# One decoder layer on one core: the first attention reads, the last head's sums and the last conv output pieces change places

## The chip, the cores and the metric

The kernel runs on one core of a Trainium2 chip. The metric is the time of one execution on the device in microseconds (us), as the median of several runs. A core has five engines with instruction queues of their own: PE (TensorE, matmuls and transposes), DVE (VectorE), ACT (ScalarE), POOL (GpSimd) and SP, which here issues all the DMAs. They wait for each other by semaphores only. Matmuls read SBUF and write PSUM; the other engines read PSUM and so make a PSUM tile free for the next matmuls.

## The reference

One transformer layer over 1024 tokens of width 1024, float32. Cut to what matters here:

```python
h = rms_norm(x, g_mix)
q, k, v, qi, ki, wi, conv_in, gate_a, gate_c = jnp.split(h @ w_in, pts, axis=-1)
q, k = per-head rms_norm                      # 8 heads of 64
# indexer: scores of every query with every key, the 256 best are kept
rel   = relu(einsum('bqhd,bsd->bqhs', qi, ki) * 64 ** -0.5)
idx   = top_k(where(causal, einsum('bqhs,bqh->bqs', rel, wi), -inf), 256)
# attention of each query over its selected keys, 8 heads
attn  = softmax(where(valid, q . k[idx] * 64 ** -0.5, -inf)) @ v[idx]
conv  = silu(layer_norm(causal depthwise conv of a * sigmoid(g), 31 taps))
x = x + (sigmoid(gate_a) * (attn @ w_attn_o)
         + sigmoid(gate_c) * (conv @ w_conv_o)) @ w_out
x = x + (silu(hf @ w_gate) * (hf @ w_up)) @ w_down        # hf = rms_norm(x)
x = x + sigmoid(rms_norm(x) @ w_pg) * (p @ w_pp)
```

## The kernel before

Everything is kept transposed, with features on the partitions and the 1024 tokens along the free axis. A large product is done with operands split in two rounded float32 parts (`..hi` and `..lo`), so that one product takes three matmuls of 128x512 (hi by hi, lo by hi, hi by lo). The stages come in this order: projection for the indexer; the search for the 256th score of each query, spread over the following stages; conv input and gates; blocks for k, v and q; attention; the merge of both branches through `w_ao` (attention output) and the gates; `w_out`; feed-forward; the last embedding product.

**q blocks.** Four q blocks (`qk_gemm(0, i)`), two heads each, come one after another. A block's product lies in a pair of PSUM banks (tag `g`, two such pairs). ScalarE squares it (`sq`), ScalarE and VectorE write its two parts `qh` and `ql`, and SP spills them to device memory (`qdh`, `qdl`, 512 KB each). Behind block i the statistics of block i-1 are made: 16 matmuls with `headsel` (L724), `ms` on VectorE, `r` on GpSimd (L205) and two small products on VectorE (`rq`, L730). The order of this part is set by a scheduler, which places each instruction by the time it simulates.

**Attention operands.** `att_prep(j)` (L758) reads the spilled q and k of two heads back, in the layout that the scores want: for each head `qst` (q's two parts one above the other), and two `kst` tiles with k's parts twice. It is 12 DMAs of 64x1024 (256 KB), all from SP, L128. In the kernel before, `att_prep(0)` stands behind q block 2.

**Attention loop.** From L952 the order is written by hand: engines run exactly what the code emits, in that order. A unit is a pair of heads j and a block b of 128 queries; 32 units run in a software pipeline over i from -2 to 32. In step i stand, for each of the two heads u: `scores(u)` of unit i+2 (L787, into a PSUM pair `g`; VectorE adds the mask and takes the maximum into `lg`, L790), a conv output piece, `turn(u)` of unit i (transposes of `lg`, L812, into PSUM tiles of tag `m`, of which there are three; ScalarE and VectorE write them to `pt`, L813 and L814), `values(u)` of unit i-1 (L826, L827) and `exp(u)` of unit i+1 (ScalarE, L802). Then `negmax` (`nmx`), and `finish` of unit i-1: a reciprocal on VectorE, two scaled copies to `osum` on ScalarE (L841), and two sums on GpSimd (L843, L844) that write `attn`. Every four units `att_turn` transposes half a head pair's result (4 transposes, L853) and `att_split` rounds it into `ahi` and `alo` on VectorE (L858, L859) for the merge. The first unit's scores and the statistics of q block 3 open the loop.

**Conv output pieces.** `co_blocks` (L863) is a generator of 64 pieces, each three matmuls into the PSUM tile `f`, of which there is one. Four pieces fill it, then VectorE multiplies it with the gate (`scl`, L881); two such halves make a spill (`cgd`). `pump(co)` emits the next piece: the loop uses them to fill TensorE between the steps (FILL gives how many for each b), and `pump(co, 64)` emits what is left after the loop. Some of those left are placed by the scheduler among the instructions of the loop's end. The matmuls of the merge (tile `g` from `ahi` and `alo`, gate product into `sal`) for the first two outputs are moved up in the same way.

Of the kernel before, what the change touches and what calls it, by code (L numbers as in the profile page):

```python
# [18 lines left out]
ALU = mybir.AluOpType  # L19
# [52 lines left out]
def tile_layer(ctx: ExitStack, tc: tile.TileContext, A, out):  # L72
    nc = tc.nc
    pe, dve, act, pool, sp = nc.tensor, nc.vector, nc.scalar, nc.gpsimd, nc.sync
# [10 lines left out]
    def nm(s):  # L85
        cnt[0] += 1
        return f"{s}_{cnt[0]}"

    def U(name="u", dt=F32, shape=(P, S)):
        return up.tile(list(shape), dt, tag="u", name=nm(name))  # L90
# [12 lines left out]
    def PM(shape=(P, 512)):  # L103
        return mp.tile(list(shape), F32, tag="m", name=nm("m"))
# [14 lines left out]
    def pump(gen, k=1):  # L119
        for _ in range(k):  # L120
            next(gen, None)
# [539 lines left out]
    def v_turn(j, vt):  # L661
        pt = PG()
        for tb in range(8):
            pe.transpose(pt[:, tb * P:(tb + 1) * P], vt[:, tb * P:(tb + 1) * P], ident)
        pv = pt.rearrange("p (t h c) -> p t h c", t=8, h=2)
        r = U("vr")
        rv = r.rearrange("p (t h c) -> p t h c", t=8, h=2)
        for u in range(2):
            vv = U("vall", BF16, (P, 8, VW))
            parts = [vv[:, :, 2 + 64 * i: 66 + 64 * i] for i in range(3)]  # L670
            act.activation(parts[0], pv[:, :, u], AF.Copy)
            dve.tensor_tensor(rv[:, :, u], pv[:, :, u], parts[0], op=ALU.subtract)

            dve.tensor_tensor(vv[:, :, 0:2], rv[:, :, u, 0:2], rv[:, :, u, 0:2], op=ALU.is_equal)
            act.activation(parts[1], rv[:, :, u], AF.Copy)
            dve.tensor_tensor(parts[2], rv[:, :, u], parts[1], op=ALU.subtract)
            vall.append(vv)
# [28 lines left out]
    def qk_gemm(which, j):  # L706
        wt = weights("w_k" if which else "w_q", j)
        ps = PG()
        gemm(halves(ps), wk(wt, 8), hT)
        sq = U("sq")  # L710
        act.activation(sq, ps, AF.Square)
        if which:
            o = U("k")
            act.activation(o, ps, AF.Copy, scale=gqk)
            return sq, o
        hi, lo = U("qh", FR), U("ql", FR)
        split_x(hi, lo, ps)
        to_dram(hi, lo, qd, "qd")
        return sq, None

    def qk_stats(sq):
        st = PM()
        for tb in range(8):
            pe.matmul(st[:, 2 * tb:2 * tb + 2], lhsT=sq[:, tb * P:(tb + 1) * P], rhs=headsel, start=True, stop=True)  # L724
        return rstd_of(st[:, 0:16], 1.0 / HD, 16)

    def q_scales(r):
        for dst, sign in ((rq, 1.0), (nrq, -1.0)):
            t = up.tile([P, 16], F32, tag="rq", name=nm("rq"), bufs=8)
            dve.tensor_scalar(t, r, sign * HD ** -0.5, None, op0=ALU.mult)  # L730
            dst.append(t)
# [24 lines left out]
    def att_prep(j):  # L756
        (qh, ql), (kh, kl) = qd[j], kd[j]
        for u in range(2):  # L758
            rows = slice(64 * u, 64 * u + 64)
            a, b0, b1 = U("qst", FR), U("kst", FR), U("kst", FR)  # L760
            mv(a[0:64], qh[rows])
            mv(a[64:128], ql[rows])
            for o in (0, 64):
                mv(b0[o:o + 64], kh[rows])
                mv(b1[o:o + 64], kl[rows])
            stk[2 * j + u] = a, b0, b1
# [3 lines left out]
    class Unit:  # L770
# [57 lines left out]
                          start=False, stop=(kb == self.b))  # L828
            self.pt[u] = None

        def finish(self):
            j = self.j
            if j not in avs:
                avs[j] = U("attn")
            avv = avs[j].rearrange("p (b h c) -> p b h c", b=8, h=2)
            o2 = self.o[:, 0:2 * VW].rearrange("p (u x) -> p u x", u=2)
            rc = up.tile([P, 2], F32, tag="s2", name=nm("rc"), bufs=12)
            dve.reciprocal(rc, o2[:, :, 0])
            sm = U("osum")[:, 0:6 * HD].rearrange("p (u i c) -> p u i c", u=2, i=3)
            for u in range(2):  # L840
                act.activation(sm[:, u], o2[:, u, 2:VW].rearrange("p (i c) -> p i c", i=3), AF.Copy,  # L841
                               scale=rc[:, u:u + 1])
            pool.tensor_tensor(sm[:, :, 1], sm[:, :, 1], sm[:, :, 2], op=ALU.add)  # L843
            pool.tensor_tensor(avv[:, self.b], sm[:, :, 0], sm[:, :, 1], op=ALU.add)  # L844

    def att_turn(j, half):
        av = avs[j]
        if len(aT) == j:
            aT.append((U("ahi", FR), U("alo", FR)))
        ps = PM()  # L850
        for i in range(4):
            c = half * 512 + i * P
            pe.transpose(ps[:, i * P:(i + 1) * P], av[:, c:c + P], ident)  # L853
        return j, half, ps

    def att_split(j, half, ps):
        hi, lo = (t[:, HV[half]] for t in aT[j])
        dve.tensor_copy(hi, ps)  # L858
        dve.tensor_tensor(lo, ps, hi.bitcast(F32), op=ALU.subtract)  # L859
# [3 lines left out]
    def co_blocks():  # L863
        def fetch(n):
            g = U("scl")
            sp.dma_start(g, spill_g[1, n])
            return g

        nxt = fetch(0)
        for n2 in range(4):  # L870
            wt = weights("w_co", n2)
            for i in range(2):
                n = 2 * n2 + i
                g = nxt
                d = dp.tile([P, S], F32, tag=f"cg{n}", name=nm("cgd"))
                for sl in HV:
                    ps = fp.tile([P, 512], F32, tag="f", name=nm("f"))
                    for k in range(4):
                        gemm([(ps, sl)], wk(wt, 4, off=512 * i), cT, k, k + 1)
                        if k == 3:  # L880
                            dve.tensor_tensor(g[:, sl], g[:, sl], ps, op=ALU.mult)  # L881
                        if sl == HV[1] and k == 0 and n < 7:
                            nxt = fetch(n + 1)
                        yield
                sp.dma_start(d, g)
                spill_c[n] = d
# [55 lines left out]
    for i in range(4):  # L942
        xq[i] = qk_gemm(0, i)
        if i == 0:
            pump(cn_)
            v_turn(3, vt.pop(3))
        else:
            q_scales(qk_stats(xq.pop(i - 1)[0]))
        if i == 2:
            att_prep(0)  # L950
        pump(cn_)
    co = co_blocks()  # L952
    todo = [(j, b) for j in range(4) for b in (range(7, -1, -1) if j % 2 == 0 else range(8))]
    N = len(todo)
    un = {}
    with tc.manual_schedule():
        for i in range(-2, N + 1):
            new, nxt, cur, old = None, un.get(i + 1), un.get(i), un.pop(i - 1, None)
            if i + 2 < N:
                new = un[i + 2] = Unit(*todo[i + 2])  # L960
            if i == 0:
                r3 = qk_stats(xq.pop(3)[0])
            if i == 2:
                q_scales(r3)
            if i % 8 == 2 and i < 24:
                att_prep(i // 8 + 1)
            fill = FILL[cur.b] if 0 <= i < N else 0
            for u in range(2):
                if new:
                    new.scores(u)  # L970
                if u < fill:
                    pump(co)
                if 0 <= i < N:
                    cur.turn(u)
                if old:
                    old.values(u)
                if nxt:
                    nxt.exp(u)
                if u + 2 < fill:
                    pump(co)  # L980
            if new:
                new.negmax()
            if old:
                old.finish()
            if i > 4 and i % 4 == 1:
                j, odd = (i - 5) // 8, (i - 5) % 8 // 4
                att_split(*att_turn(j, (1 - odd) if j % 2 == 0 else odd))
    pump(co, 64)
    att_split(*att_turn(3, 1))


    mhi, mlo, sg_, cg_ = [], [], {}, {}
# [421 lines left out]
```

## Time and profile before

| | |
|---|---|
| median of 3 runs | 1629.14 us (1626.28 to 1632.62) |
| profiled execution | 1629.16 us |
| its span in the trace | 1627.3 us |
| mean granted clock of TensorE | 0.991 |
| TensorE busy | 1590.6 us (98% of the span) |
| VectorE, ScalarE, GpSimd busy | 70%, 44%, 9% |
| DMA moved | 184.69 MB, 113 GB/s on average |

Times in the trace count from the start of the span. The q blocks run from about 493 to 540 us, the attention loop from 540 to 723 us, the merge from there on. Busy time of a group of matmuls is modelled, since they are pipelined: the start of the next group says when it made room. The granted clock is a share of full speed (1.00 is 2.4 GHz, 0.50 is 1.2 GHz). An idle time stands in brackets behind the instruction that ended it, with what released it.

### The profile page before, as it was taken

Reading aid. Unit: us, or ns where it says so; the run is one execution under the profiler, and the core shown is the slowest. Engines: PE = TensorE matmul, PEld = TensorE weight load, DVE = VectorE, ACT = ScalarE, POOL = GpSimd, SP = SyncE. Lnnn points to the kernel's source line nnn. Section 1 sums busy time; section 2 is a strip of 40 time slices with the busy share of each in tenths; the row PEclk is TensorE's granted clock in tenths of the full one; section 3 lists DMA queues with packets and bytes.
Section 4 is the critical chain, followed back from the end, with each engine's and each line's share of the span. In section 5 each row is a group of like instructions: output and inputs, shape, how many; then the busy total and the mean of one; then the engine's idle time right before and its main releaser. Section 6 shows DMA issues by size and latency. Waiting matters only on the chain.

```text
span 1627.3 us, 20334 instructions
## 1 busy us (share of the span) xinstructions
PE 1590.6 (98%) x7736; PEld 1329.4 (82%) x7736; DVE 1140.8 (70%) x1804; ACT 714.2 (44%) x1066; POOL 150.1 (9%) x136
## 2 busy tenths in 40 slices
PE   8999999999999999999999899999999999999998
PEld 6888888888878788878888678888888888888887
DVE  5669999884899778747468876667777544437763
ACT  5456375768733577742234433322322322212531
POOL 2101100000202521221001200000000000000210
PEclk9999999999999899999999999999999999999999
DMA  7330222232221844336542122222222552223254
GB/s 290 95 91 27 65 91 89 94 104 78 91 91 72 225 131 110 103 145 223 210 136 78 59 78 87 93 80 78 78 78 91 182 193 83 99 91 104 92 199 136
DMA packets 61538, 184.69 MB, mean 113 GB/s; under 512 B 7296, under 2 KB 7808, under 8 KB 61440
## 3 DMA queue, kind: packets, MB, share of 16 engines
q1 hardware_dynamic: 61440, 183.38, 33.9%
q8 instruction: 61, 1.00, 0.3%
q14 instruction: 37, 0.30, 0.1%
HBM read 134.60 MB, written 45.09 MB: 110 GB/s over the span
## 4 chain that ended last, share of the span: by engine, by line
PE 52%; DVE 3%; ACT 0%; issue 0%; ACTq 0%; DVEq 0%
PE g L190 41%; PE m L190 10%; DVE xsum L1080 1%; DVE xc L179 0%; DVE wlo L179 0%; DVE wd L1153 0%; PE m L212 0%; DVE h L248 0%; PE f L190 0%; ACT whi L178 0%; DVE sil L1127 0%; PE m L222 0%; ACT one L178 0%; DVE raw L1157 0%; DVE sal L1010 0%
## 5 line engine op out<-in xcount | busy, mean ns | idle before, releaser
L143 ACT ACTIVATE whi<-raw 128x1024 fp32r<-128x1024 f32 x110 | 115.5, 1051 | 199.5 <-PE g L190 182.4
L190 PE MATMUL g<-hhi,whi 128*128 128x512 f32 (+2 forms) x656 | 201.0, 388 | 2.1 <-ACT vt L658 1.5
L190 PE MATMUL g<-hlo,whi 128*128 128x512 f32 (+2 forms) x656 | 199.5, 385 | 2.6 <-POOL hlo L179 1.3
L190 PE MATMUL g<-hhi,wlo 128*128 128x512 f32 (+2 forms) x656 | 199.3, 385 | 0.0
L144 DVE TENSOR_TENSOR wlo<-raw,whi 128x1024 fp32r<-128x1024 f32 x102 | 127.3, 1249 | 44.9 <-ACT whi L143 44.7
L613 DVE SCALAR_TENSOR_TENSOR cacc<-glu,vecs,cacc 128x994 f32<-128x994 f32 (+14 forms) x120 | 151.7, 1264 | 2.7 <-ACT cacc L610 1.9
L511 ACT ACTIVATE junka<-Y,tr 128x1024 bf16<-128x1024 f32 (+3 forms) x128 | 126.3, 987 | 46.0 <-DVE tr L536 23.1
L190 PEld LDWEIGHTS g<-hlo,whi 128*128 128x128 f32 (+1 forms) x656 | 122.2, 187 | 28.0 <-POOL hlo L179 2.1
L190 PEld LDWEIGHTS g<-hhi,whi 128*128 128x128 f32 (+1 forms) x656 | 121.6, 187 | 25.4 <-ACT vt L658 1.9
L190 PEld LDWEIGHTS g<-hhi,wlo 128*128 128x128 f32 (+1 forms) x656 | 122.2, 187 | 24.2
L1292 DVE TENSOR_TENSOR x<-x,g 128x1024 f32<-128x1024 f32 (+1 forms) x56 | 59.8, 1067 | 107.7 <-PE g L190 107.7
L205 POOL TENSOR_TENSOR r<-ms,mhalf 128x16 f32<-128x16 f32 (+2 forms) x14 | 34.8, 2489 | 1036.2 <-DVE ms L203 1020.6
L190 PE MATMUL g<-xc,whi 128*128 128x512 f32 x352 | 109.9, 394 | 4.7 <-DVE sil L1127 3.3
L190 PE MATMUL g<-fah,whi 128*128 128x512 f32 x352 | 113.9, 390 | 0.4 <-ACT phi L178 0.4
L190 PE MATMUL g<-fal,whi 128*128 128x512 f32 x352 | 113.6, 389 | 0.0
L190 PE MATMUL g<-fah,wlo 128*128 128x512 f32 x352 | 113.6, 389 | 0.0
L190 PE MATMUL g<-xc,w 128*128 128x512 f32 x480 | 112.0, 389 | 0.0
L190 PE MATMUL m<-xc,whi 128*128 128x512 f32 x352 | 108.9, 390 | 0.0
L190 PEld LDWEIGHTS g<-xc,w 128*128 128x128 f32 x480 | 90.0, 188 | 18.8 <-ACT w L178 0.2
L190 PEld LDWEIGHTS g<-xc,whi 128*128 128x128 f32 x352 | 66.7, 190 | 19.5 <-DVE sil L1127 3.7
L190 PEld LDWEIGHTS g<-fah,whi 128*128 128x128 f32 x352 | 66.1, 188 | 14.6 <-ACT phi L178 0.7
L814 DVE SCALAR_TENSOR_TENSOR pt<-m,pt 128x512 f16<-128x512 f32 (+3 forms) x96 | 50.6, 554 | 38.9 <-ACT pt L813 38.4
(240 smaller groups left out, 3226.6 us busy)
## 6 DMA issues: line engine op xcount, KB each, us to landing
raw<-w_fd SPq DMA_DIRECT2D x26, 512.0 KB, 3.8
hd<-hd SPq DMA_DIRECT2D x22, 512.0 KB, 4.9
raw<-w_fg SPq DMA_DIRECT2D x40, 256.0 KB, 3.0
raw<-w_fu SPq DMA_DIRECT2D x40, 256.0 KB, 2.9
hd<-c SPq DMA_DIRECT2D x20, 512.0 KB, 2.8
x<-xT SPq DMA_DIRECT2D x16, 512.0 KB, 8.5
sgd<-sg SPq DMA_DIRECT2D x16, 512.0 KB, 2.9
raw<-w_out SPq DMA_DIRECT2D x16, 512.0 KB, 3.8
```

The lines of the kernel that those rows point to most:

```text
L143: act.activation(hi, raw, AF.Copy)
L144: lo_eng.tensor_tensor(lo, raw, hi.bitcast(F32), op=ALU.subtract)
L190: pe.matmul(ps, lhsT=W[k][wi], rhs=X[k][xi][:, sl], start=(k == 0 and t == 0), stop=(k == K - 1 and t == 2))
L205: pool.tensor_tensor(r, ms, mhalf[:, :width], op=ALU.pow)
L511: act.activation(junka[:, :n], ysl(b), AF.Sign, scale=-1.0, bias=self.tr[:, c], accum_out=self.cn[:, c])
L613: dve.scalar_tensor_tensor(acc[:, sl], g, w, acc[:, sl], op0=ALU.mult, op1=ALU.add)
L814: dve.scalar_tensor_tensor(lo[:, c0:c0 + cw], pt[:, :cw], PSCALE, hi[:, c0:c0 + cw], op0=ALU.mult, op1=ALU.subtract)
L1080: dve.tensor_tensor(a, x2[p + k][:, HV[u]], x2[q + k][:, HV[v]], op=op)
L1292: dve.tensor_tensor(x2[n][:, sl], x2[n][:, sl], ps[:, sl], op=ALU.add)
```

## The change

It has three parts. `att_prep(0)` is emitted behind q block 1 instead of q block 2. `finish` gets the engine for its two sums as an argument: GpSimd as before, but VectorE for the last unit. And at the end of the hand-ordered part now stand four conv output pieces, the last `att_turn`, three pieces and the last `att_split`; before, the remaining pieces and both calls stood behind that part.

```diff
@@ -828,7 +828,7 @@
                           start=False, stop=(kb == self.b))
             self.pt[u] = None
 
-        def finish(self):
+        def finish(self, add):
             j = self.j
             if j not in avs:
                 avs[j] = U("attn")
@@ -840,8 +840,8 @@
             for u in range(2):
                 act.activation(sm[:, u], o2[:, u, 2:VW].rearrange("p (i c) -> p i c", i=3), AF.Copy,
                                scale=rc[:, u:u + 1])
-            pool.tensor_tensor(sm[:, :, 1], sm[:, :, 1], sm[:, :, 2], op=ALU.add)
-            pool.tensor_tensor(avv[:, self.b], sm[:, :, 0], sm[:, :, 1], op=ALU.add)
+            add.tensor_tensor(sm[:, :, 1], sm[:, :, 1], sm[:, :, 2], op=ALU.add)
+            add.tensor_tensor(avv[:, self.b], sm[:, :, 0], sm[:, :, 1], op=ALU.add)
 
     def att_turn(j, half):
         av = avs[j]
@@ -946,7 +946,7 @@
             v_turn(3, vt.pop(3))
         else:
             q_scales(qk_stats(xq.pop(i - 1)[0]))
-        if i == 2:
+        if i == 1:
             att_prep(0)
         pump(cn_)
     co = co_blocks()
@@ -981,12 +981,15 @@
             if new:
                 new.negmax()
             if old:
-                old.finish()
+                old.finish(dve if i == N else pool)
             if i > 4 and i % 4 == 1:
                 j, odd = (i - 5) // 8, (i - 5) % 8 // 4
                 att_split(*att_turn(j, (1 - odd) if j % 2 == 0 else odd))
+        pump(co, 4)
+        last = att_turn(3, 1)
+        pump(co, 3)
+        att_split(*last)
     pump(co, 64)
-    att_split(*att_turn(3, 1))
 
 
     mhi, mlo, sg_, cg_ = [], [], {}, {}
```

The first place is SP's queue at q blocks 1 and 2. `qdh_4135` and `qdl_4137` are the spill of block 1; `qdh_4230` and `qdl_4232` that of block 2 in the kernel before. Before:

```order
L128 DMA qdh_4135<-qh_4131 128x1024
L128 DMA qdl_4137<-ql_4132 128x1024
L128 DMA qdh_4230<-qh_4226 128x1024
L128 DMA qst_4251<-qdh_4008 64x1024
L128 DMA qst_4251<-qdl_4010 64x1024
L128 DMA qdl_4232<-ql_4227 128x1024
L128 DMA kst_4252<-kdh_3471 64x1024
...
L128 DMA kst_4262<-kdl_3473 64x1024
L128 DMA qdh_4368<-qh_4364 128x1024
```

After, where `qdh_4248` and `qdl_4250` are the spill of block 2:

```order
L128 DMA qdh_4135<-qh_4131 128x1024
L128 DMA qst_4156<-qdh_4008 64x1024
L128 DMA qst_4156<-qdl_4010 64x1024
L128 DMA qdl_4137<-ql_4132 128x1024
L128 DMA kst_4157<-kdh_3471 64x1024
L128 DMA kst_4158<-kdl_3473 64x1024
...
L128 DMA kst_4167<-kdl_3473 64x1024
L128 DMA qdh_4248<-qh_4244 128x1024
L128 DMA qdl_4250<-ql_4245 128x1024
L128 DMA qdh_4368<-qh_4364 128x1024
```

Two of the twelve reads stand ahead of the second half of block 1's spill, the other ten behind it, and both halves of block 2's spill behind all twelve.

The second place is TensorE at the end of the loop, from the first transposes of the last unit (`m_6667`) on. `chi`, `clo` are the conv branch's operand, `whi`, `wlo` the weights. `pt_6600` is unit 30's, `m_6681` its values. Before, the last unit's transposes, a group of twelve `f` matmuls (its middle left out) and then the values of unit 30:

```order
L190 MATMUL f_6479<-chi_4303,wlo_6000 128x512
L812 MATMUL m_6667<-ident_73,lg_6519 128x128 x4
L812 MATMUL m_6674<-ident_73,lg_6519 128x128 x4
L190 MATMUL f_6773<-chi_4288,whi_5999 128x512
L190 MATMUL f_6773<-clo_4289,whi_5999 128x512
...
L190 MATMUL f_6773<-clo_4304,whi_5999 128x512
L190 MATMUL f_6773<-chi_4303,wlo_6000 128x512
L826 LDWEIGHTS pt_6600
L826 MATMUL m_6681<-vall_4033,pt_6600 128x194
```

After, the same place, and further on in the queue the last four transposes of `attn` (`m_6788`) between two groups of `f`:

```order
L812 MATMUL m_6667<-ident_73,lg_6519 128x128 x4
L812 MATMUL m_6674<-ident_73,lg_6519 128x128 x4
L826 LDWEIGHTS pt_6600
L826 MATMUL m_6681<-vall_4033,pt_6600 128x194
...
L190 MATMUL f_6772<-clo_4304,whi_5999 128x512
L190 MATMUL f_6772<-chi_4303,wlo_6000 128x512
L853 MATMUL m_6788<-ident_73,attn_6294 128x128 x4
L190 MATMUL f_6795<-chi_4288,whi_5999 128x512
...
L190 MATMUL f_6795<-chi_4303,wlo_6000 128x512
L190 MATMUL g_6845<-ahi_6588,whi_6472 128x512
```

The group of twelve between the first transposes and the values of unit 30 is gone from there, and so is another one ahead of unit 31's values. One group now stands ahead of the last four transposes and one between these and the merge's first products from `ahi`. A third one, which stood between those products, comes behind them.

The third place is VectorE there, from the first transposes' copies to the gate products. Before:

```order
L814 SCALAR_TENSOR_TENSOR pt_6666<-m_6667,pt_6666 128x512
L814 SCALAR_TENSOR_TENSOR pt_6666<-m_6674,pt_6666 128x512
L881 TENSOR_TENSOR scl_6346<-scl_6346,f_6773 128x512
L814 SCALAR_TENSOR_TENSOR pt_6696<-m_6697,pt_6696 128x512
L814 SCALAR_TENSOR_TENSOR pt_6696<-m_6704,pt_6696 128x512
L838 RECIPROCAL rc_6725<-m_6681 128x2
L838 RECIPROCAL rc_6765<-m_6732 128x2
L858 CAST ahi_6588<-m_6820 128x512
L881 TENSOR_TENSOR scl_6777<-scl_6777,f_6791 128x512
L859 TENSOR_TENSOR alo_6589<-m_6820,ahi_6588 128x512
L881 TENSOR_TENSOR scl_6777<-scl_6777,f_6805 128x512
L1010 TENSOR_TENSOR sal_6827<-sal_6827,g_6845 128x1024
```

After:

```order
L814 SCALAR_TENSOR_TENSOR pt_6666<-m_6667,pt_6666 128x512
L814 SCALAR_TENSOR_TENSOR pt_6666<-m_6674,pt_6666 128x512
L814 SCALAR_TENSOR_TENSOR pt_6696<-m_6697,pt_6696 128x512
L814 SCALAR_TENSOR_TENSOR pt_6696<-m_6704,pt_6696 128x512
L838 RECIPROCAL rc_6725<-m_6681 128x2
L838 RECIPROCAL rc_6765<-m_6732 128x2
L843 TENSOR_TENSOR osum_6767<-osum_6767 128x2x64
L844 TENSOR_TENSOR attn_6294<-osum_6767 128x128
L881 TENSOR_TENSOR scl_6346<-scl_6346,f_6772 128x512
L858 CAST ahi_6588<-m_6788 128x512
L859 TENSOR_TENSOR alo_6589<-m_6788,ahi_6588 128x512
L881 TENSOR_TENSOR scl_6776<-scl_6776,f_6795 128x512
```

The product L881 between the two pairs of L814 is gone from there, the two sums stand behind the reciprocals, and a L881 stands ahead of `ahi` and behind `alo`.

## Rows read from the trace of the kernel before

**Rows 1.** Page, busy time: us (share of the span), instructions.
```profile
PE 1590.6 (98%) x7736; PEld 1329.4 (82%) x7736; DVE 1140.8 (70%) x1804; ACT 714.2 (44%) x1066; POOL 150.1 (9%) x136
```

**Rows 2.** Stretches: length, busy us by engine, granted clock, DMA share, GB/s.
```profile
496.00:497.00 1.00, 1.00 (x10) 1.00 (x8) 1.00 (x2) 0.00 (x0) 0.00 (x0) 0.75 0.78 152
545.00:557.00 12.00, 11.70 (x39) 10.21 (x40) 5.05 (x13) 3.32 (x3) 5.62 (x3) 0.50 0.69 231
558.00:570.00 12.00, 12.00 (x114) 11.22 (x113) 9.97 (x25) 10.31 (x18) 2.25 (x3) 1.00 0.88 198
722.00:727.00 5.00, 2.38 (x20) 1.82 (x18) 1.83 (x4) 0.73 (x2) 0.90 (x2) 1.00 1.02 419
```

**Rows 3.** Timeline of TensorE, start of attention: start, us, instruction [idle <-releaser].
```profile
538.73 1.84 PE L724 MATMUL m<-headsel,sq 128*128 128x2 f32 x16
540.43 1.19 PE L787 MATMUL g<-kst,qst 128*128 128x512 f32 x4
545.30 5.23 PE L787 MATMUL g<-kst,qst 128*128 128x512 f32 x12 [3.68 <-DMA kst<-kdh]
...
556.31 1.84 PE L812 MATMUL m<-ident,lg 128*128 128x128 f32 x8
...
558.69 0.38 PE L812 MATMUL m<-ident,lg 128*128 128x128 f32 x2
```

**Rows 4.** Timeline of SP's DMA issues, q blocks 1 to 3.
```profile
515.13 0.33 SPq L128 DMA_DIRECT2D qdh<-qh  x1
519.40 0.32 SPq L128 DMA_DIRECT2D qdl<-ql  x1
527.36 0.32 SPq L128 DMA_DIRECT2D qdh<-qh  x1
527.77 0.48 SPq L128 DMA_DIRECT2D qst<-qdh  x1
...
536.38 0.44 SPq L128 DMA_DIRECT2D kst<-kdl  x1
```

**Rows 5.** DMA from 527 to 546; and landing of tile kst, 520 to 600.
```profile
DMA packets 1390, 4.75 MB, mean 250 GB/s; under 512 B 231, under 2 KB 231, under 8 KB 1389
...
DMA to landing us min/median/max: 3.4/6.3/9.7
```

**Rows 6.** Timeline of VectorE and GpSimd, start of attention.
```profile
535.16 5.18 DVE L643 CAST chi<-cacc 128x1024 fp32r<-128x1024 f32 x2 [0.43 <-ACT cacc L641]
...
540.90 1.22 DVE L179 TENSOR_TENSOR ql<-g,qh 128x1024 fp32r<-128x1024 f32 x1
542.04 1.21 DVE L790 CUSTOM_DVE_ANT_0 lg<-g,bias 128x1024 f32<-128x1024 f32 x1
...
544.83 2.89 POOL L205 TENSOR_TENSOR r<-ms,mhalf 128x16 f32<-128x16 f32 x1
```

**Rows 7.** Timeline of TensorE, end of attention.
```profile
711.85 0.50 PE L190 MATMUL f<-chi,whi 128*128 128x512 f32 x1
...
714.71 0.26 PE L826 MATMUL m<-vall,pt 128*128 128x194 bf16 x1
...
715.71 1.04 PE L812 MATMUL m<-ident,lg 128*128 128x128 f32 x8
...
724.98 0.33 PE L853 MATMUL m<-ident,attn 128*128 128x128 f32 x1 [1.83 <-POOL attn L844]
726.09 0.50 PE L190 MATMUL g<-ahi,whi 128*128 128x512 f32 x1 [0.79 <-DVE ahi L858]
...
732.00 0.50 PE L190 MATMUL g<-ahi,whi 128*128 128x512 f32 x1 [0.63 <-DVE sal L1010]
```

**Rows 8.** Timeline of VectorE and GpSimd, end of attention.
```profile
712.45 1.29 DVE L814 SCALAR_TENSOR_TENSOR pt<-m,pt 128x512 f16<-128x512 f32 x2 [0.65 <-ACT pt L813]
714.91 0.69 DVE L881 TENSOR_TENSOR scl<-scl,f 128x512 f32<-128x512 f32 x1 [1.18 <-PE f L190]
...
723.94 0.45 POOL L843 TENSOR_TENSOR osum<-osum 128x128 f32<-128x128 f32 x1 [3.70 <-ACT osum L841]
```

## The prediction

> **What bounds the kernel now.** The first view to read is the page's table of busy time: TensorE is busy for 1590.6 of 1627.3 us [rows 1]. So only about 37 us can be had by filling its gaps, and more only where it runs below full speed. The second view is therefore the table of stretches, for the granted clock [rows 2]: TensorE stands at 0.50, the lower of its two levels (1.2 GHz), from 545 to 557, and at 1.00 from 558 on. The third is TensorE's own timeline around that stretch [rows 3]. At 545.30 twelve score matmuls (the first unit's second head, both heads of the second unit) start after 3.68 us of idling that ended with the landing of a `kst` read; the twelve take 5.23 us. Four such matmuls took 1.19 us at 540.43, so twelve are worth some 3.6 at full clock. The loss of this place is thus in two parts: the wait, and the slow stretch behind it. The DMA queue's timeline says why the read is late: the first read of the twelve is issued at 527.77, the last at 536.38, and a `kst` read lands between 3.4 and 9.7 us after its issue [rows 4, 5].
>
> The second place is the end of the attention loop [rows 7]. TensorE stops for 1.83 us (until GpSimd's second sum is written), for 0.79 (until VectorE has rounded `ahi`) and for 0.63 (until VectorE's product with the gate frees a PSUM tile): 3.25 us. The clock stays at 1.00 there, although TensorE is busy for 2.38 of 5 us [rows 2].
>
> **Part 1, the reads one block earlier.** Nothing is added or removed; twelve DMAs of 262 KB move ahead in SP's order. They now stand behind the spill of q block 1 (issued 515.13 and 519.40) and ahead of the two spills of q block 2 [rows 4]. What they read, k's first spill and q block 0's, was written before that. So the first two go at about 515.5, and the other ten follow `qdl(1)` at 519.4. They took 536.38 - 527.77 = 8.6 us to issue with one spill among them; ten take about 7, from 519.8 to 527. By the rate of the stretch in which they run now (250 GB/s [rows 5]), ten reads and the 0.52 MB spill ahead of them are 3.14 MB or 12.6 us: landed by 532. By the longest landing of any `kst` read (9.7 us) it is 537. Either is ahead of 540.43, when the first scores run. So the wait of 3.68 goes.
>
> What is late next is VectorE. The second head's scores need the PSUM pair that `ql` of q block 3 is still read from, and that operation runs 540.90 to 542.12 [rows 6]. From there I rebuild the order with full-clock durations:
> - second head's scores 542.12 to 543.31 (1.19 [rows 3]), where they began at 545.30;
> - the third group needs the first `lg` out of PSUM, 542.04 + 1.21 = 543.25 [rows 6]: no wait, to 544.50;
> - the fourth needs the second `lg`, 543.31 + 1.21 and a hop: it begins at 544.6 and ends at 545.8;
> - statistics of q block 3, 540.43 - 538.73 = 1.70 in q block 2's group of the same size: 547.5; fifth scores (768 columns of 1024, at most 0.9): 548.4;
> - three conv output matmuls, 0.7 (twelve take 714.71 - 711.85 = 2.86 [rows 7]): 549.1.
>
> The transposes of the first unit start there, instead of at 556.31: 7.2 us. They and the scores up to 558.69 take 2.38 us in the trace, of which the first 1.84 is a group that takes 1.04 at full clock [rows 3, 7]: 1.8 at most with the small waits, so 550.9 against 558.69. **Part 1 gives 7.8 us**: 3.2 from the wait, 4.6 from the clock.
>
> Where could it be given back? Two waits move onto VectorE and GpSimd. GpSimd's `r` of q block 2 ends at 544.83 + 2.89 = 547.72 [rows 6], and VectorE's two `rq` that read it now stand ahead of a `nmx`, a `ms` and the third unit's first `lg`. They cost VectorE some 0.8 us behind the fourth `lg` (546.9), while TensorE is in the statistics and fifth scores: the fifth `lg` starts at 548.4 anyhow. If that cover fails, it is 0.8 at most. And the spill of q block 2 now stands behind all twelve reads: VectorE's third `chi` (535.16 [rows 6]) overwrites a tile that this spill reads, so it waits for its landing. At 250 GB/s that is 532.0 + 2.1 = 534.1, 1.06 us early; with the longest landing, 9.7 us from its issue at 527.4, it is 537.1, 1.9 us late. A delay x there moves `chi`, `ql` and the second scores by x. I take no delay, since the rate is that of the same transfers; the other end keeps 1.9 us in the range.
>
> **Part 2, the last unit's sums on VectorE.** Two GpSimd instructions of 0.45 us [rows 8] become two on VectorE. The trace has no such operation on VectorE with 64 columns; the nearest is the product of 128x512 at 0.69 us [rows 8], four times the columns, so both together cost between 0 and 1.38. I take about 0.6, and it doesn't matter: twelve `f` matmuls, 2.86 us, now run on TensorE meanwhile.
>
> **Part 3, conv output pieces between.** No matmul is added. Two groups of twelve leave the places before `values(30,0)` (unit 30, head 0) and before `values(31,0)`, and one stands ahead of the last four transposes, one ahead of the last `ahi`/`alo` products, and the third moves from between those products to behind them. Waits left, by my reckoning:
> - the last unit's second transposes need PSUM that VectorE frees at 712.45 + 0.65 and + 1.29; TensorE would be there at 711.85 + 1.0 = 712.85, the values' 715.71 - 714.71 being 1.0 [rows 7, 8]: 0.25, and 0.2 for the second four;
> - behind the sums, the transposes are covered by `f`: 2.86 us against a chain of reciprocal, two ScalarE copies and the sums of under 2.5: 0.1;
> - the next `f` group needs the only `f` tile, which VectorE frees 0.69 us after the group ahead [rows 8]; four transposes cover 0.5 of it: 0.45 with the hops between engines;
> - `ahi` and `alo` lie under twelve `f`, and so does the gate's product: 0.
>
> That is 1.0 us where 3.25 stood: **2.2 us**. Bounds: all three waits may go (3.25), or the fillers taken away may uncover more (0).
>
> **Sum.** 7.8 + 2.2 = 10.0 us off the profiled execution's 1629.16, which is the median of the three runs as well (1629.14): **1619.2 us**, 0.6% less. This kernel's runs can tell about 0.5% from no change, 8.1 us: below 1621.0 is faster.
>
> **Rivals.**
> *A: the clock falls nevertheless.* Between the score groups TensorE still pauses for VectorE, 0.6 us at first and 0.1 later, and switches tiles each time. If the gate still closes here, the slow stretch stays and only the wait goes: 3.2 + 2.2 = 5.4, or 1623.8. Against it speaks 722 to 727, with 2.62 us of idling in five at 1.00; for it, that 496 to 497 shows 0.75 with TensorE busy throughout [rows 2], so that not only long waits are followed by a fall. The Trainium skill ("TensorE: Matmul & The Clock Gate", section "A second HAM failure mode: psum-queue depth-cycling") says that short stalls while cycling through PSUM tiles make the clock swing. No row here shows that by itself. 0.13.
> *B: the tail gives nothing.* The two groups taken away covered the evacuation of the transposes in PSUM, 1.29 us twice; if each is bare, 2 us come back: 1621.4. For it speaks that VectorE's row at 712.45 ends 0.9 us after TensorE would be free; against it, that each four transposes need only one half of it. 0.10.
> *C: the wait only moves, and the reads give nothing.* Something else than the reads holds the second scores to about 545: only the tail is left, 1629.2 - 2.2 = 1627.0. Against it speaks that the wait is on `kst` by the trace and that VectorE has done both things these scores need from it by 542.12. 0.05.
> *D, slower: the spill behind the reads.* If qdh(2) lands x late, `chi`, `ql` and the scores wait; the clock falls again from x = 3.2 on, which takes part 1 whole; it is slower than before from x = 5.4, a landing at 540.6, 13.2 us after its issue. At x = 8 it is 1629.2 + 4.8 - 2.2 = 1631.8. The longest read shown is 9.7 [rows 5]. The Trainium skill ("DMA: Bandwidth & Descriptors", section "Queues, rings and completion order") says that a ring's descriptors are taken in order, and that a completion shows only behind all earlier writes of that DMA engine; so the spill would pay for all of the backlog ahead of it. No row here shows a spill behind a dozen reads. 0.03.
>
> **How the numbers follow.** The forecast has 0.66, with its own range of 1616.5 (3.25 in the tail, and part 1 without its small waits and hops) to 1621.5 (most of 0.8 and 1.9 us given back). Better than that has 0.03. The range of 8 in 10, with rival A and B in it for the most part: 1615.5 to 1624.5. Faster by over 0.5%: most of the forecast's 0.66 (0.62), the 0.03, and some of B: 0.68. Within 0.5%: A, C, most of B, and a twentieth from the forecast's upper end: 0.28. Slower: D and a little beside: 0.04.
>
> **What would show it.** In TensorE's timeline of after, no wait for `kst` ahead of the second scores, a granted clock of 1.00 (not 0.50) through the next 13 us, and the first transposes some 7 us earlier than 556.31. On SP, twelve reads between the spills of q blocks 1 and 2. On VectorE, the third `chi` without a wait for a DMA. In the tail no wait for `attn`, `ahi` or `sal`, and a short one behind the last transposes' group. It is wrong if the clock row stays at 0.50 (A), if a wait on `qdh` shows on VectorE (D), or if TensorE waits for `pt` at the end (B).

## The result and the profile after

The changed kernel takes 1621.30 us as the median of 6 runs (1619.42 to 1623.18), beside 1630.41 for the kernel before: a ratio of 0.9944, 95% interval 0.9928 to 0.9961, or 9.1 us less. A second set of five runs gave 1620.69 beside 1628.41: 0.9955 (0.9941 to 0.9969), 7.7 us less. Forecast were 10.0 us less than 1629.16. The profiled execution took 1619.42 us, its span is 1617.5.

TensorE's timeline at the start of attention, changed kernel (it answers to [rows 3]; start, us, instruction, in brackets the idle time before it and what ended it):

```profile
539.17 1.84 PE L724 MATMUL m<-headsel,sq 128*128 128x2 f32 x16
540.87 1.19 PE L787 MATMUL g<-kst,qst 128*128 128x512 f32 x4
542.67 2.17 PE L787 MATMUL g<-kst,qst 128*128 128x512 f32 x8 [0.60 <-PE g L787]
545.16 1.07 PE L787 MATMUL g<-kst,qst 128*128 128x448 f32 x4 [0.32 <-DVE mx L790]
546.07 1.84 PE L724 MATMUL m<-headsel,sq 128*128 128x2 f32 x16
547.77 0.95 PE L787 MATMUL g<-kst,qst 128*128 128x384 f32 x4
...
549.25 1.03 PE L812 MATMUL m<-ident,lg 128*128 128x128 f32 x8
```

The wait for `kst` is gone; what is left is 0.60 and 0.32 for VectorE (the 0.60 ends with its `ql`, below: 541.34 + 1.22 = 542.56). From the first scores to the first transposes it was 556.31 - 540.43 = 15.88 us, and it is 549.25 - 540.87 = 8.38. SP's queue says that the reads went where they were forecast to go ([rows 4]: `qdh` of block 1, first read; spill of block 2 behind the last read):

```profile
515.57 0.33 SPq L128 DMA_DIRECT2D qdh<-qh  x1
516.06 0.48 SPq L128 DMA_DIRECT2D qst<-qdh  x1
...
526.90 0.59 SPq L128 DMA_DIRECT2D kst<-kdl  x1
527.80 0.33 SPq L128 DMA_DIRECT2D qdh<-qh  x1
```

VectorE in the same stretch ([rows 6]):

```profile
536.26 4.51 DVE L643 CAST chi<-cacc 128x1024 fp32r<-128x1024 f32 x2 [1.09 <-DMA qdh<-qh]
541.05 0.17 DVE L203 TENSOR_SCALAR ms<-m 128x16 f32<-128x16 f32 x1 [0.28 <-PE m L724]
541.34 1.22 DVE L179 TENSOR_TENSOR ql<-g,qh 128x1024 fp32r<-128x1024 f32 x1
...
548.25 0.25 DVE L730 TENSOR_SCALAR rq<-r 128x16 f32<-128x16 f32 x2 [0.85 <-POOL r L205]
```

Both new waits are there, 1.09 us for the spill behind the reads and 0.85 for GpSimd's `r`, and neither moves the end: behind the first, VectorE still waits 0.28 us for TensorE's statistics, and `ql` starts 0.47 us behind the first scores, as before (541.34 - 540.87, and 540.90 - 540.43).

At the end of the loop, TensorE's timeline ([rows 7]):

```profile
703.19 1.03 PE L812 MATMUL m<-ident,lg 128*128 128x128 f32 x8
...
705.46 1.25 PE L812 MATMUL m<-ident,lg 128*128 128x128 f32 x8
...
712.65 0.60 PE L853 MATMUL m<-ident,attn 128*128 128x128 f32 x4
713.59 0.50 PE L190 MATMUL f<-chi,whi 128*128 128x512 f32 x1 [0.34 <-DVE scl L881]
...
721.44 0.61 PE L190 MATMUL g<-ahi,whi 128*128 128x512 f32 x2
```

and VectorE's ([rows 8]):

```profile
711.15 0.29 DVE L843 TENSOR_TENSOR osum<-osum 128x128 f32<-128x128 f32 x1 [0.95 <-ACT osum L841]
711.47 0.29 DVE L844 TENSOR_TENSOR attn<-osum 128x128 f32<-128x128 f32 x1
712.85 0.69 DVE L881 TENSOR_TENSOR scl<-scl,f 128x512 f32<-128x512 f32 x1 [1.08 <-PE f L190]
```

The waits for `attn`, `ahi` and `sal` are gone; 0.34 us for `f` are left, and 0.3 ahead of the last unit's second transposes (705.46 - 703.19 = 2.27 us, for 0.9 of transposes and 1.0 of values). In the kernel before, the last unit's first transposes start here, and the merge's third output at 732.00 [rows 7]:

```profile
710.91 1.03 PE L812 MATMUL m<-ident,lg 128*128 128x128 f32 x8
```

That is 21.09 us; now it is 721.44 - 703.19 = 18.25, 2.84 us less.

Last, the granted clock, in stretches of the changed kernel ([rows 2]; the clock is the third number from the end):

```profile
545.00:557.00 12.00, 11.84 (x95) 11.10 (x96) 9.86 (x26) 9.76 (x14) 8.47 (x4) 1.00 1.00 253
712.00:717.00 5.00, 4.66 (x23) 3.66 (x22) 2.33 (x4) 0.00 (x0) 0.00 (x0) 1.00 0.26 105
891.00:900.00 9.00, 5.74 (x14) 4.45 (x14) 3.35 (x7) 1.39 (x3) 0.00 (x0) 0.62 0.44 146
```

The two changed places run at full clock. The third row is a place that the change doesn't touch, behind a wait of 3.26 us in the feed-forward part.

### The profile page after: what moved, and what is told of

Its sections match the earlier page's. It is cut to its first block, busy times and chain, and to the rows that moved or that the text cites. A ratio compares the mean times of both kernels' runs of the same rounds, so it can differ in the third digit from the quotient of the medians.

```text
span 1617.5 us, 20344 instructions
## 1 busy us (share of the span) xinstructions
PE 1585.9 (98%) x7736; PEld 1325.4 (82%) x7736; DVE 1142.0 (71%) x1806; ACT 714.4 (44%) x1066; POOL 148.7 (9%) x134
## 4 chain that ended last, share of the span: by engine, by line
PE 89%; DVE 7%; ACT 2%; issue 1%; DMA 1%; POOL 0%; SPq 0%; ACTq 0%; DVEq 0%; POOLq 0%
PE g L190 67%; PE m L190 10%; PE f L190 2%; PE g L787 2%; PE m L443 2%; PE m L812 2%; PE m L826 1%; DVE xsum L1083 1%; PE m L724 1%; PE m L827 1%; DVE xc L179 0%; DVE wlo L144 0%; PE m L212 0%; ACT pt L813 0%; DVE pt L814 0%
## 5 line engine op out<-in xcount | busy, mean ns | idle before, releaser
L190 PEld LDWEIGHTS g<-fah,wlo 128*128 128x128 f32 x352 | 66.1, 188 | 13.8
```

The lines of the kernel that those rows point to most:

```text
L190: pe.matmul(ps, lhsT=W[k][wi], rhs=X[k][xi][:, sl], start=(k == 0 and t == 0), stop=(k == K - 1 and t == 2))
```

## The experiments

**One part alone.** The reads alone are the kernel before with this edit, the tail alone is the changed kernel without it:

```diff
-        if i == 2:
+        if i == 1:
             att_prep(0)
```

> Only the twelve reads go one q block earlier; sums and conv output pieces as before. Theory (the wait and the slow clock behind it are both the reads'): about 8 us less than before (0.995), the first transposes of the first unit near 549 instead of 556.3, granted clock 1.00 from 545 to 557, and the three waits of 3.25 us at the end of the loop as they were. Rival A (the clock falls all the same between the score groups): 3.2 us less, clock 0.50 there. Rival (the gain seen is the tail's for the most part): under 4 us less.

Measured: 1624.28 us (11 runs) beside 1628.30, ratio 0.9978 (0.9969 to 0.9987), 4.0 us less by the medians, half of what was expected. Yet in its trace the place itself is just as forecast: 8.38 us from first scores to first transposes, at a clock of 1.00. Beside the first trace of the kernel before, this execution loses 1.7 us in the first 40 us, nearly all of it by a clock of 0.79 from 26 to 34 us (1.00 there in the other), and 1.6 at the end of the loop, which this kernel leaves as before. TensorE's timeline there:

```profile
718.56 0.33 PE L853 MATMUL m<-ident,attn 128*128 128x128 f32 x1 [1.84 <-POOL attn L844]
719.68 0.50 PE L190 MATMUL g<-ahi,whi 128*128 128x512 f32 x1 [0.78 <-DVE ahi L858]
...
727.18 0.73 PE L190 MATMUL g<-ahi,whi 128*128 128x512 f32 x2 [0.64 <-DVE sal L1010]
```

And the stretch around these waits, with its clock:

```profile
718.00:723.00 5.00, 3.65 (x11) 2.76 (x12) 1.89 (x3) 0.00 (x0) 0.46 (x1) 0.76 0.69 280
```

The waits are those of [rows 7], but the clock falls to 0.76 here, and from the transpose to the third output it takes 727.18 - 718.56 = 8.62 us instead of 732.00 - 724.98 = 7.02. That accounts for this execution, not for the average of 11: the kernel before has the same waits there, and its second trace, further on, shows the same fall.

> Only the sums and the pieces at the end of the loop; the reads stand behind q block 2 as before. Theory: the wait for kst of about 3.7 us and the granted clock of 0.50 from 545 to 557 are back; between the last unit's first transposes and the merge's third output 2.8 us less than the 21.1 of before, so 2 to 3 us less than before in all (0.998 to 0.9985). Rival B (the tail gives nothing, what it saves comes back as waits for PSUM): no difference, 1.000.

Measured: 1624.18 us (11 runs) beside 1628.30, ratio 0.9977 (0.9968 to 0.9986), 4.1 us less (2.3 to 5.2 by the interval), against 2 to 3 expected. The tail is the changed kernel's: 18.26 us from the last unit's first transposes to the merge's third output. The wait for `kst` and the slow stretch are back, 15.73 us from first scores to first transposes:

```profile
541.73 1.19 PE L787 MATMUL g<-kst,qst 128*128 128x512 f32 x4
546.46 5.23 PE L787 MATMUL g<-kst,qst 128*128 128x512 f32 x12 [3.53 <-DMA kst<-kdh]
...
557.46 1.84 PE L812 MATMUL m<-ident,lg 128*128 128x128 f32 x8
```

The two halves add up to 8.1 us by the medians, about what the whole change gives (7.7 and 9.1).

**TensorE busy during the wait.** The kernel before, with 28 transposes of the identity in front of the first unit's second scores:

```diff
                 if new:
                     new.scores(u)
+                if i == -2 and u == 0:
+                    wm = PM()
+                    for c in range(28):
+                        pe.transpose(wm[:, c % 4 * P:c % 4 * P + P], ident, ident)
```

> The kernel before, with 28 transposes of the identity into a PSUM tile that nobody reads, between the first unit's two score groups, so that TensorE has work during the wait for kst. The wait itself stays. Theory (two prices: 3.2 us of wait, and some 4.6 us of slow clock that come from the idling): the second scores start at about 545.3 as before, granted clock 1.00 behind them, first transposes near 552 instead of 556.3, 4 to 5 us less than before (0.997). Rival (the clock falls because of the score and statistics groups themselves, not because of the idling): clock 0.50 as before, no difference.

In this trace, TensorE's timeline is the theory's:

```profile
543.81 1.19 PE L787 MATMUL g<-kst,qst 128*128 128x512 f32 x4
544.84 3.22 PE L974 MATMUL m<-ident 128*128 128x128 f32 x28
548.51 2.33 PE L787 MATMUL g<-kst,qst 128*128 128x512 f32 x8 [0.46 <-DMA kst<-kdh]
...
555.46 1.04 PE L812 MATMUL m<-ident,lg 128*128 128x128 f32 x8
...
557.04 1.09 PE L812 MATMUL m<-ident,lg 128*128 128x128 f32 x8
```

The second scores start 4.70 us behind the first, as before (4.87), the clock is 1.00 behind them, and it takes 11.65 us to the first transposes (555.46) instead of 15.88: 4.2 us are the clock's, and 11.65 - 8.38 = 3.27 are the wait's. But the time is 1627.63 us beside 1628.30, ratio 0.9991 (0.9981 to 1.0001): 1.5 us by the ratio, not the 4 to 5 expected. So an average execution of the kernel before doesn't lose what the profiled one lost here. The mean granted clock, which is known for every execution, says so too: 0.9918 on average over the 27 of the kernel before, 0.9937 over these 11. Of 1628 us that is some 3.1 us at most; at most, since a low clock costs nothing while TensorE idles. By the same count the reads alone (0.9931) save at most 2.1 us of slow clock, and the tail alone (0.9921) at most 0.5.

**The kernel before once more.**

> The kernel before once more, for a second trace of it. Theory (what the traces disagree on outside the changed places is not the change's): the first 40 us differ from the first trace of before by up to some us, the wait for kst (3.5 to 3.7 us) and the granted clock of 0.50 behind it are there again, the waits of 1.8, 0.8 and 0.6 us at the end of the loop too, while the clock there may be 1.00 or about 0.8, as in the run with the reads alone. Rival (the start's offset belongs to each program): the second wait for phi at 0.68 us and the first 40 us as in the first trace, to 0.1 us.

It took 1628.58 us. TensorE's timeline at the start of attention, the same program, the same wait:

```profile
542.89 1.19 PE L787 MATMUL g<-kst,qst 128*128 128x512 f32 x4
547.31 4.55 PE L787 MATMUL g<-kst,qst 128*128 128x512 f32 x12 [3.23 <-DMA kst<-kdh]
551.70 1.84 PE L724 MATMUL m<-headsel,sq 128*128 128x2 f32 x16
...
554.88 1.04 PE L812 MATMUL m<-ident,lg 128*128 128x128 f32 x8
```

The price is another one. I had expected the clock of 0.50 again; three stretches of this trace show:

```profile
545.00:550.00 5.00, 2.69 (x7) 1.94 (x8) 1.36 (x3) 0.00 (x0) 5.00 (x3) 0.76 1.02 329
550.00:555.00 5.00, 5.00 (x32) 4.32 (x31) 4.01 (x12) 3.33 (x3) 1.29 (x2) 0.90 0.92 283
722.00:727.00 5.00, 3.40 (x10) 2.55 (x11) 1.89 (x3) 0.00 (x0) 0.69 (x2) 0.81 0.70 284
```

The statistics run at full clock (1.84, where [rows 3] stand in a stretch at 0.50), and it is 11.99 us from the first scores to the first transposes: the slow stretch costs 0.3 us here, not 4.2. (Counted from the second scores on it is 7.57 us, against 6.95 with the wait filled, so 0.6: this wait was 0.3 us shorter.) The end of the loop, at 1.00 in [rows 2], shows 0.81, and costs the 1.6 us of the kernel with the reads alone. The start of the program is 2.4 us later too, by other waits for its first operands and by a clock of 0.79 from 26 to 34 us, where the first trace has 1.00. The rival, that a program has its own dips and start, falls.

**The parts of the tail.** The changed kernel with the sums on GpSimd again (`old.finish(pool)`):

> The changed kernel, but the last unit's two sums on GpSimd as before. Theory: twelve conv output matmuls (2.85 us) cover reciprocal, copies and the sums on either engine, so the last transposes start no more than 0.2 us later than in the changed kernel behind the loop's last values (5.0 us from the first f to the merge's next f group), and the time is the changed kernel's within 1 us. Rival (the engine of the sums is what takes the 1.83 us away): a wait for attn of 0.4 to 1 us comes back ahead of the last four transposes.

Measured: 1619.80 us (4 runs), ratio 0.9944 (0.9927 to 0.9960), no different from the changed kernel. GpSimd's sums end at 712.01, the twelve `f` matmuls still cover them, as TensorE's timeline shows:

```profile
712.53 0.60 PE L853 MATMUL m<-ident,attn 128*128 128x128 f32 x4
713.47 0.50 PE L190 MATMUL f<-chi,whi 128*128 128x512 f32 x1 [0.34 <-DVE scl L881]
```

And without the pieces, with the two lines behind the loop as before:

```diff
-        pump(co, 4)
-        last = att_turn(3, 1)
-        pump(co, 3)
-        att_split(*last)
     pump(co, 64)
+    att_split(*att_turn(3, 1))
```

> Reads early and the sums on VectorE, but the conv output pieces where they were. Theory: the wait for attn goes from 1.83 to about 1.3 us, those for ahi (0.8) and sal (0.6) stay, 2.7 us in all, and the granted clock behind them may fall as it did with the reads alone (0.76): 4 to 7 us less than before, so 2 to 5 more than the changed kernel. Rival (the sums alone are enough): within 1 us of the changed kernel.

Measured: 1624.68 us (10 runs), ratio 0.9976 (0.9964 to 0.9987); in the same runs the kernel before took 1628.13, so of the 4 to 7 us expected 3.5 came (2.1 to 5.9 by the interval), and the kernel with the sums on GpSimd took 1619.80, 4.9 us less. TensorE's timeline at the end of the loop:

```profile
717.55 0.33 PE L853 MATMUL m<-ident,attn 128*128 128x128 f32 x1 [1.50 <-DVE attn L844]
718.67 0.50 PE L190 MATMUL g<-ahi,whi 128*128 128x512 f32 x1 [0.78 <-DVE ahi L858]
...
724.59 0.73 PE L190 MATMUL g<-ahi,whi 128*128 128x512 f32 x2 [0.64 <-DVE sal L1010]
```

The engine of the sums is worth 0.3 us of wait (1.50 for 1.83) and nothing once the pieces stand there; the order of the pieces is what takes the waits away. In the traces that is 2.5 of the 4.9 us (from the last unit's first transposes to the third output 20.78 us here, 18.25 with the sums on GpSimd); the mean granted clock of these executions, 0.9934 beside 0.9948, can give 2.2 more at most.

**Other waits filled.** The changed kernel with transposes that nobody reads, in three more waits:

```diff
+    def warm(count, src=None):
+        wm = fp.tile([P, 512], F32, tag="f", name=nm("f"))
+        for c in range(count):
+            pe.transpose(wm[:, c % 4 * P:c % 4 * P + P], ident if src is None else src[:, c % 8 * P:c % 8 * P + P], ident)
...
+        warm(12, t1)
         rep = replicate(mu, 8)
...
-        gate_up(FIRST[0], hs[0], 1, B12 + xs(5), (None, one_of(3), lambda: pair_make(ms[0])))
+        gate_up(FIRST[0], hs[0], 1, B12 + xs(5),
+                (None, lambda: (warm(26), one_of(3)()), lambda: pair_make(ms[0])))
...
-        gated(ms[0], strassen(ms[0], {4: six_seven(0), 5: six_seven(2), 1: lambda: pair_make(ms[1], pool)}))
+        gated(ms[0], strassen(ms[0], {4: six_seven(0), 5: six_seven(2), 3: lambda: warm(23), 1: lambda: pair_make(ms[1], pool)}))
```

> The changed kernel with transposes into PSUM that nobody reads in three waits that it leaves as they are: 12 before the conv norm's mean is there (wait for mu, 1.6 us, clock 0.59 to 0.73 behind it), 26 in the wait for sil (3.26 us, clock 0.50 behind it), 23 in the wait for one (2.85 us, clock 0.71). Theory (idling is what lowers the clock, in other places too): granted clock 1.00 in all three, the waits unchanged in length with the transposes in them, mean clock 0.998 or more, and 5 to 8 us less than the changed kernel, about 1614. Rival (the clock falls there because of the groups of 128x1 and 128x2 matmuls and the norm, not the idling): clock as in the changed kernel, within 1 us of it.

Measured: 1618.62 us (6 runs), ratio 0.9935 (0.9921 to 0.9949): 1.2 us less than the 1619.80 of the kernel with the sums on GpSimd in the same runs, far from 5 to 8. Behind `mu` the clock stays up, and the way from the q blocks to the first scores is 3.2 us shorter (56.9 us from the last wait for `vt`, 60.1 before). The 26 for `sil` I had put in the wrong place: they ran at 870, ahead of a gate product for which TensorE had not been waiting, so this product and VectorE's work on it came later, and the wait for `sil` ended 1.5 us later behind the merge's third output than in the changed kernel (174.33 us for 172.86); and this execution's clock fell to 0.70 from 545 to 550. The next kernel moves the 26 behind `product(p25[:, L], 2)` in the first Strassen product, where the wait is, and puts 5 ahead of the first unit's second scores. With it ran the changed kernel again.

> The changed kernel once more, for more runs and a second trace. Theory (the waits are the program's, the slow clock behind a wait is each execution's): 0.9935 to 0.9955 of before, the start of the loop without the wait for kst; of the clock's dips those behind mu, sil and one again, and perhaps a short one between the first scores, where the first trace has 1.00 and that of the kernel with transposes in three waits 0.70 to 0.96. Rival (a program's dips are its own): dips at the same places and as deep as in the first trace, 1.00 between the first scores.

> As the kernel with transposes in three waits, but the 26 for sil stand where TensorE does wait for it (inside the first Strassen product, behind its first quarter, instead of ahead of a gate product that then came 3 us late), and 5 more in the wait of 0.6 us between the first head's scores and the second's. Theory: the waits for sil, one and mu and the first scores at a granted clock of 1.00, mean clock 0.998; the transposes delay nothing, so 4 to 7 us less than the changed kernel, about 1615. Rival (the time after the norm is VectorE's, not TensorE's): what TensorE gains at mu and the scores is lost in a longer wait for sil, no more than 2.5 us less than the changed kernel.

The changed kernel: 1620.69 us (5 runs). Its second trace has the waits of the first, but not its clock, as three stretches of it show:

```profile
540.00:545.00 5.00, 4.39 (x25) 3.60 (x24) 4.13 (x5) 3.22 (x3) 5.00 (x3) 0.81 0.41 165
545.00:550.00 5.00, 5.00 (x29) 4.31 (x28) 3.93 (x11) 2.96 (x3) 4.03 (x3) 0.84 1.05 309
550.00:555.00 5.00, 5.00 (x27) 4.58 (x25) 2.37 (x5) 2.32 (x4) 5.00 (x2) 0.67 0.49 115
```

No wait here is over 0.6 us, TensorE is busy for 14.39 of 15, and the clock falls all the same. It takes 10.12 us from the first scores to the first transposes instead of 8.38:

```profile
541.70 1.19 PE L787 MATMUL g<-kst,qst 128*128 128x512 f32 x4
...
551.82 1.79 PE L812 MATMUL m<-ident,lg 128*128 128x128 f32 x8
```

The kernel with the transposes moved: 1614.82 us (1613.52 to 1616.52, 5 runs), ratio 0.9917 (0.9904 to 0.9929), as the theory said; 5.9 us below the changed kernel's median in the same runs, so it beats both. The stretches with transposes in them:

```profile
495.00:505.00 10.00, 9.77 (x69) 8.85 (x70) 10.00 (x18) 4.69 (x7) 0.00 (x0) 1.00 0.42 159
540.00:552.00 12.00, 11.62 (x71) 9.79 (x71) 9.99 (x22) 7.98 (x11) 11.49 (x5) 1.00 0.90 264
885.00:895.00 10.00, 9.57 (x56) 8.16 (x55) 7.64 (x11) 4.13 (x7) 0.00 (x0) 1.00 0.17 44
908.00:920.00 12.00, 10.22 (x43) 7.51 (x42) 10.05 (x11) 3.41 (x4) 3.21 (x2) 1.00 0.20 62
```

All four places stand at 1.00, also the last, with 1.8 us of waits left in it. The transposes do none of the kernel's work: 66 of them in 1614.82 us buy back more than they cost. Which of the four places gives how much was not tried one by one. At the first scores the 1.00 says little, since of the six traces with the pause of 0.6 us left empty four stand at 1.00 as well; behind `mu`, `sil` and `one` the clock fell in every one of the nine traces without transposes there.

## Why the prediction was right, and where it was not

- **The wait for `kst`: right.** 3.2 us were forecast, 3.27 measured (11.65 with the wait at full clock, 8.38 without). The operands were in time (the last read landed 8.2 us after its issue at 526.90, so at 535.1, between the 532 and the 537 reckoned), and VectorE was next, as written: the first transposes came 7.5 us earlier than before behind the first scores, where 7.2 were forecast.
- **The clock behind it: the step that failed, by its size.** "4.6 from the clock" was read from a single execution. For that one it was about right: up to the second group of transposes, where it was counted, 558.69 - 540.43 = 18.26 against 557.04 - 543.81 = 13.23 with the wait filled, 5.0 us. But four traces have this wait with TensorE idle or filled: up to the first transposes the slow stretch cost 4.2 us in the first (15.88 against 11.65), as much in the tail-only kernel (15.73), and 0.3 to 0.6 in the second trace of the kernel before. The filled wait, which takes the clock's share alone away, gained 1.5 us on average, with an interval from nothing to 3.1, and 3.1 is also the most that the mean clocks allow. That is why the reads alone gained 4.0 us and not 8: 3.27 of wait, and a clock term of at most 2.1 in place of 4.6.
- **Rival A was half true.** The changed kernel's clock was 1.00 here in its first trace and fell in its second (1.7 us). A pause of 0.6 us was followed by a fall in one execution and not in the other. I had given it 0.13 as one case or the other; it differs from execution to execution. What decides it, the pause or something else, no run separates.
- **The tail: right in kind, too small.** 2.2 forecast, 2.84 in the trace: of the waits I left in, 0.3 and 0.34 are there where 0.45 and 0.45 were reckoned, and the groups of `f` cost nothing where they went; the last tenths of the difference I did not trace. What I took from [rows 2], that the clock stays up there, held in the kernel before's first trace, with the wait for `kst` filled and without the pieces, but not in the kernel before's second trace nor with the reads alone, and then the waits cost 1.6 more. So it fell in two of the five traces with these waits, and in none of the six without them: 0.6 us on average, in line with the 0.5 of the mean clocks. With 2.84 that makes 3.4, and the 4.1 of the tail alone lie within its interval of that.
- **The sum: right within its range, in part by luck.** The medians, 1621.30 and 1620.69, lie at the slow end of the forecast's own 1616.5 to 1621.5, since a clock term that was too large met a tail that was too small. 3.27 + 2.84 = 6.1 us are waits, which the executions share. The rest, up to the measured 9.1 and 7.7, fits the clock: its mean rose from 0.9918 to 0.9938 and 0.9934 in the two sets of the changed kernel, 3.3 and 2.6 us at most. The filled wait gives 1.5 of it at the first place and the five traces some 0.6 at the second; neither share is known to better than a microsecond or so.
- **Part 2: right.** "It doesn't matter" is what the kernel with the sums on GpSimd shows. One sum takes 0.29 us on VectorE, 0.6 for both as estimated.
- **The waits that were moved: right in their cost, wrong in one step.** VectorE waits 0.85 us for `r`, where 0.8 were reckoned, under the statistics and fifth scores. The spill of block 2 landed 8.3 us after its issue at 527.80, so at 536.1 and not by 534.1: the third `chi` waited 1.09 us for it. That is rival D's first step, and one of the signs by which I would have called the forecast wrong. It cost nothing because the two `chi` then took 4.51 us instead of 5.18, and TensorE's statistics end behind them anyway. I had written that a delay x there moves `ql` and the second scores by x; this one moved neither.

## What to carry to other kernels

Read an idle time of TensorE as two prices: the wait, which each execution pays, and a slow stretch behind it, which can differ from one execution to the next; price the second over several traces or by the mean granted clock of many executions, or measure it by giving TensorE idle work during the wait. Here the two parts added up when each was measured alone over many runs (8.1 us beside 7.7 and 9.1); prices read from one trace did not. When filler matmuls can be put around a dependent chain, look first at where they stand, and only then at which engine does the chain's small steps.

## What the runs showed that I had not expected

- The same program's slow stretch behind the same wait of 3.2 to 3.7 us cost 4.2 us in one execution and 0.3 to 0.6 in the next; the waits of 1.8, 0.8 and 0.6 us cost 0 or 1.6 more.
- Transposes whose result nobody reads keep the clock at 1.00 through waits of 1.6 to 3.3 us, behind which it had fallen in all nine traces without them; 66 of them gained 5.9 us.
- Time that TensorE gains can be lost again at a place that another engine bounds: filler of 3 us one product too early moved VectorE's next product, and with it the end of the wait.
- The first 40 us differ by up to 3.4 us between traces, by the waits for the first operands and by a fall of the clock between 26 and 34 us in some of them (0.79 for 1.00); a change of some us is not to be read from the absolute times of two traces, only from stretches inside them.
